# Quarter-block products mixed with whole ones, weight sums by accumulating transfers, and stored low parts, in a decoder layer on one core

## The chip, the cores and the metric

The kernel runs on one core of one Trainium2 chip, as one program. The time is the device time of one execution in microseconds; before the change it is the median of three runs. The engines are named as in the profile: PE (TensorE matmuls, with PEld for its weight loads), DVE (VectorE), ACT (ScalarE), POOL (GpSimd) and SP (SyncE). SP and POOL issue the transfers here, each in the order of its own queue (q1 in the profile is SP's queue, q0 POOL's); both run on the same 16 DMA engines.

## The reference

One layer, 2048 tokens of width 1024, in float32:

```python
h = x * (1.0 + sc1) + sh1                      # sc, sh, g: from cond @ w_ada + b_ada
z = h @ w_in[l]                                # 1024 -> 2048
y_conv = gate_b * _short_conv(gate_c * v_conv, conv_w[l])
y_pool = _multiscale_pool(v_pool, w_pool[l], pool_scale[l])
mix = jnp.concatenate([y_conv, y_pool], axis=-1) @ w_out[l]
x = _layer_norm(ALPHA * x + (1.0 + g1) * mix, ln1_g[l], ln1_b[l])
h = x * (1.0 + sc2) + sh2
f = jnp.square(jax.nn.relu(h @ w_mlp_in[l])) @ w_mlp_out[l]   # 1024 -> 4096 -> 1024
x = _layer_norm(ALPHA * x + (1.0 + g2) * f, ln2_g[l], ln2_b[l])
```

## The kernel before

The tokens go through in two blocks of 1024 (`b` 0 and 1). Each block passes the input projection, the convolution and pooling, the output projection with the first normalisation, the up-projection in eight groups of 512 hidden channels (`up`), and the down-projection with the second normalisation (`down`).

Every float32 operand is split into a high and a low part (`split`: a copy on ACT, line 81, and a subtraction on DVE, line 82), and a product takes three matmuls (`mm3`, lines 86 to 88): high by high, high by low, low by high. Most of the large products are done as seven half-size products in place of eight, in the manner of Strassen and Winograd. `ORDER` lists the seven: number 0 is block 11 by block 11, 1 is 12 by 21, 2 to 5 take sums s1 to s4 of the left operand's blocks and sums 1 to 3 of the weights, or block 22, and 6 takes block 22 and sum 4. Sums of weights are made once, by loading four blocks, four DVE operations and four stores.

In the second block's down-projection three of the seven products (`FINE`: 1, 5 and 3, here numbered n = 0, 1, 2) are cut once more into seven, so that they become 21 parts with matmuls of 256 columns (line 1139). Their left operands are quarter blocks that `up` stores in `uquart` as it goes (`save_quarters`). Their weight sums, `wquart`, are made by `sum_quarters` during the second block's up-projection: `QUARTER_SUMS` says how many of the twelve calls follow each group. A call loads four half rows on SP (line 980) into two `o` tiles, makes four DVE operations (line 91) and stores four results on POOL (line 992). The weights of n = 0 and 1 are an input (`w2q`); those of n = 2 are the first block's weight sums (`w2sum`).

The second block's down-projection runs product 0 in two halves of four groups, then the 21 parts one behind the other, then products 2, 4 and 6, each in two halves. In its second half such a product goes tile by tile (`by_tile`), so that each of the four output tiles ends, and is added and normalised, while the next one is multiplied. Product 0, 2, 4 and 6 share four banks, on which each adds to what stands there; the parts use three others. Loads of operands run one half, or two parts, ahead.

`residual` loads the eight saved rows of the first normalisation (`nsave`) on SP into `r` tiles, scales and shifts them on DVE, and stores them (`rsave`) on POOL. It is driven in four turns of two rows from `down`.

The order on each engine is not only that of the source. The framework lists the program's instructions by readiness and priority and gives each engine a fixed list; `issue_after` holds an instruction back behind another one of its engine. On the chip each engine works its list in order and waits where an operand, a tile or a place among its outstanding transfers isn't there. Tiles come from pools of fixed size: 28 `h` tiles for split operands, 12 `o`, 6 `w`, 5 `r`, of 512 KiB each, and 8 banks `ps`.

The first input projection (`first_group`) opens the program: for each of eight steps SP loads two rows of `wada`, a strip of `win0` and one of `xT` (line 101), DVE makes the dot products for scale and shift and the low parts, and PE does 24 matmuls (line 402). POOL's first transfer is a row of `wada` for a later scale (line 205).

## Time and profile before

| | |
|---|---|
| median of 3 runs | 1771.32 us (1770.84 to 1772.63) |
| profiled execution | 1769.99 us, span 1768.2 us |
| PE busy | 1733.0 us (98%), 8132 matmuls |
| DVE, ACT, POOL busy | 1374.6, 887.1, 253.6 us |
| transferred | 497 MB; q1 324 MB, q0 171 MB |
| DMA engines' share, first 60 us / 60 to 200 us | 0.97 / 0.92 |

The page gives busy time by engine; the view by stretches gives, for each stretch, its length and then for each engine the busy time and in brackets the count of instructions, the granted TensorE clock (1.00 is full), the share of the 16 DMA engines that was in use, and GB/s. The view of waits gives who waited for whom: total, times, longest. A row of the timeline is start, length, engine, line, operation, output and input tiles; in brackets the idle time before and what ended it. A group's row gives count, busy time and mean ns of one, then the idle time before them.

### The profile page before, as it was taken

Reading aid. Unit: us, or ns where it says so; the run is one execution under the profiler, and the core shown is the slowest. Engines: PE = TensorE matmul, PEld = TensorE weight load, DVE = VectorE, ACT = ScalarE, POOL = GpSimd, SP = SyncE. Lnnn points to the kernel's source line nnn. Section 1 sums busy time; section 2 is a strip of 40 time slices with the busy share of each in tenths; the row PEclk is TensorE's granted clock in tenths of the full one; section 3 lists DMA queues with packets and bytes.
Section 4 is the critical chain, followed back from the end, with each engine's and each line's share of the span. In section 5 each row is a group of like instructions: output and inputs, shape, how many; then the busy total and the mean of one; then the engine's idle time right before and its main releaser. Section 6 shows DMA issues by size and latency. Waiting matters only on the chain.

```text
span 1768.2 us, 22793 instructions
## 1 busy us (share of the span) xinstructions
PE 1733.0 (98%) x8132; PEld 1453.7 (82%) x8132; DVE 1374.6 (78%) x1820; ACT 887.1 (50%) x1206; POOL 253.6 (14%) x469
## 2 busy tenths in 40 slices
PE   9999999999999999999999999999999999799997
PEld 8888888888888888888888888888877778799886
DVE  7997788877677866677786887887777668888895
ACT  5322368544445555445763345855444362666451
POOL 0222220123222000000000010112333221000000
PEclk9999999999999999999999999999999999899999
DMA  9899766788888997877653384755777799999781
GB/s 386 337 346 331 297 239 247 293 298 329 322 327 298 402 395 290 316 250 249 215 190 114 107 286 161 262 217 219 273 269 266 271 381 386 382 347 342 262 299 48
DMA packets 159841, 497.27 MB, mean 281 GB/s; under 512 B 18544, under 2 KB 26224, under 8 KB 159728
## 3 DMA queue, kind: packets, MB, share of 16 engines
q1 hardware_dynamic: 110768, 324.36, 50.5%
q0 software_dynamic: 48960, 171.47, 25.3%
q8 instruction: 63, 1.03, 0.2%
q14 instruction: 50, 0.41, 0.1%
HBM read 339.00 MB, written 156.76 MB: 280 GB/s over the span
## 4 chain that ended last, share of the span: by engine, by line
PE 82%; DVE 6%; DMA 5%; issue 4%; SPq 2%; ACT 1%; POOL 0%; DVEq 0%; ACTq 0%; POOLq 0%
PE ps L87 24%; PE ps L86 24%; PE ps L88 24%; PE ps L1139 6%; DVE o L91 3%; PE ps L402 2%; SPq L980 2%; DMA o<-in_w2q 1%; DVE w L82 1%; DMA r<-in_w 1%; DMA o<-w2sum 1%; PE ps L753 1%; DVE r L91 1%; DVE h L82 1%; DMA rsave<-r 0%
## 5 line engine op out<-in xcount | busy, mean ns | idle before, releaser
L86 PE MATMUL ps<-h,w 128*128 128x512 f32 x1312 | 511.7, 391 | 9.9 <-ACT o L1006 9.9
L88 PE MATMUL ps<-h,w 128*128 128x512 f32 x1312 | 512.1, 391 | 1.5 <-DVE w L82 1.5
L87 PE MATMUL ps<-h,w 128*128 128x512 f32 x1312 | 511.8, 390 | 0.0
L86 PE MATMUL ps<-h,h 128*128 128x512 f32 x928 | 361.8, 390 | 0.0
L88 PE MATMUL ps<-h,h 128*128 128x512 f32 x928 | 361.6, 390 | 0.0
L87 PE MATMUL ps<-h,h 128*128 128x512 f32 x928 | 361.5, 390 | 0.0
L81 ACT CAST h<-r 128x1024 fp32r<-128x1024 f32 (+1 forms) x202 | 205.5, 1021 | 243.9 <-PE ps L87 118.0
L82 DVE TENSOR_TENSOR h<-r,h 128x1024 fp32r<-128x1024 f32 (+1 forms) x202 | 238.6, 1186 | 80.8 <-ACT h L81 80.1
L86 PEld LDWEIGHTS ps<-h,w 128*128 128x128 f32 x1312 | 246.9, 188 | 63.2 <-ACT o L1006 11.6
L88 PEld LDWEIGHTS ps<-h,w 128*128 128x128 f32 x1312 | 247.1, 188 | 53.7 <-DVE w L82 2.7
L87 PEld LDWEIGHTS ps<-h,w 128*128 128x128 f32 x1312 | 247.2, 188 | 51.5 <-DVE h L82 0.4
L81 ACT CAST w<-r 128x1024 fp32r<-128x1024 f32 x156 | 163.5, 1052 | 224.2 <-PE ps L87 217.4
L82 DVE TENSOR_TENSOR w<-r,w 128x1024 fp32r<-128x1024 f32 x156 | 190.2, 1222 | 87.1 <-ACT w L81 86.4
L91 DVE TENSOR_TENSOR o<-o,o 128x512 f32<-128x512 f32 (+2 forms) x246 | 200.2, 823 | 25.0 <-DMA usum<-o 18.6
L86 PEld LDWEIGHTS ps<-h,h 128*128 128x128 f32 x928 | 174.3, 188 | 36.2 <-DVE o L91 0.3
L88 PEld LDWEIGHTS ps<-h,h 128*128 128x128 f32 x928 | 174.3, 188 | 36.1
L87 PEld LDWEIGHTS ps<-h,h 128*128 128x128 f32 x928 | 174.3, 188 | 35.9
L82 DVE TENSOR_TENSOR h<-w,h 128x1024 fp32r<-128x1024 f32 x130 | 158.7, 1221 | 11.5 <-ACT h L81 11.4
L91 DVE TENSOR_TENSOR o<-o,ps 128x512 f32<-128x512 f32 (+1 forms) x174 | 112.9, 657 | 54.9 <-PE ps L88 50.4
L1139 PE MATMUL ps<-h,h 128*128 128x256 f32 x1008 | 130.0, 293 | 12.9 <-DVE h L82 6.9
L1139 PEld LDWEIGHTS ps<-h,h 128*128 128x128 f32 x1008 | 127.9, 201 | 15.0 <-DVE h L82 8.0
L81 ACT CAST h<-w 128x1024 fp32r<-128x1024 f32 x130 | 136.5, 1050 | 6.4 <-DMA w<-in_w 4.9
(148 smaller groups left out, 1418.3 us busy)
## 6 DMA issues: line engine op xcount, KB each, us to landing
usum<-o POOLq DMA_DIRECT2D x88, 512.0 KB, 4.0
r<-usum SPq DMA_DIRECT2D x88, 512.0 KB, 5.4
w<-w2sum SPq DMA_DIRECT2D x62, 512.0 KB, 6.2
r<-in_w SPq DMA_DIRECT2D x60, 512.0 KB, 6.0
r<-uquart SPq DMA_DIRECT2D x42, 512.0 KB, 6.4
o<-in_w SPq DMA_DIRECT2D x72, 256.0 KB, 5.8
w2sum<-o POOLq DMA_DIRECT2D x64, 256.0 KB, 5.8
w<-in_w SPq DMA_DIRECT2D x32, 512.0 KB, 6.0
```

The source lines that it names most:

```text
L81: high = nc.scalar.copy(hi, src)
L82: return high.ins, nc.vector.tensor_tensor(lo, src, hi.bitcast(F32), op=ALU.subtract).ins
L86: nc.tensor.matmul(ps, whi, xhi, start=first, stop=False, skip_group_check=goes_on)
L87: nc.tensor.matmul(ps, whi, xlo, start=False, stop=False, skip_group_check=goes_on)
L88: nc.tensor.matmul(ps, wlo, xhi, start=False, stop=last, skip_group_check=goes_on)
L91: return nc.vector.tensor_tensor(out_, a, b_, op=op)
L402: nc.tensor.matmul(ps[m, h], wt[:, w : w + P], A[k][p // 2][:, hs], start=k == 0 and p == 0, stop=k == KD - 1 and p == 2)
L753: nc.tensor.transpose(ps[:, t * P : t * P + P], R[4 * h + t][:, k * P : k * P + P], ident)
L980: nc.sync.dma_start(r, weight_quarter(n, i, hf, some))
L1139: nc.tensor.matmul(ps, a[:, us], w[:, gs], start=not begun, stop=hf == 1 and g == 3 and a is ul, skip_group_check=True)
```

## The change

- **Mixed order.** In the second block's down-projection products 0 and 2 are issued by single groups of 512 channels, two times eight of them, and mixed with the 21 parts by a string (`MIX`, 1 is a group, 0 a part). Operands are made ahead as long as no more than 28 `h` tiles are held. Product 2 ends with its last group, no longer tile by tile. Products 4 and 6 follow as before.
- **Weight sums by transfers.** `sum_quarters` no longer loads, adds and stores: for each product n it issues, from POOL, eight plain copies from HBM to HBM (step 0) and eight copies that add to what stands at the target (steps 1 to 3, `accum_op`). Since these only add, some signs change: s1 and s4 of the quarter blocks, and how three of the parts are added to the output (`fine_less`, `fine_from`). The calls stand in the source in the second block's input projection (`SUM_TURNS`) and output projection. A call that adds waits for the step before it.
- **Stored low parts.** In the first block, the low parts of the weights of products 4 and 6 (16 tiles) are stored (`wlow`, POOL); in the second they are loaded on SP in place of the DVE subtraction.
- **Residual rows** of the second block are loaded from POOL's queue into `o` tiles, in place of SP and `r` tiles.

```diff
-QUARTER_SUMS = (0, 1, 2, 2, 2, 2, 2, 1)
+MIX = "1110101010101000100100100101001001001"
...
+            for n, step in SUM_TURNS[j]:
+                sum_quarters(n, step)
...
+    SUM_TURNS = (((0, 0),), ((1, 0), (0, 1)), ((2, 0), (1, 1), (0, 2)), ((2, 1), (1, 2), (0, 3)))
...
+        if b:
+            sum_quarters(2, 2)
+            sum_quarters(1, 3)
         matmuls(4, Y, False, every, first_row)
...
+        if b:
+            sum_quarters(2, 3)
         matmuls(6, X, False, every, last_row)
...
-    def sum_quarters(n, hf, part_):
-        a, b_ = t_o(T), t_o(T)
-        b22, b12, b11, b21 = a[:, :H], a[:, H:], b_[:, :H], b_[:, H:]
-        for i, r in ((3, b22), (1, b12), (0, b11), (2, b21)):
-            load_quarter(r, n, i, hf, slice(2 * part_, 2 * part_ + 2))
-        tt(b22, b22, b12, ALU.subtract)
...
+    SUM_STEPS = (((0, 1), (2, 1), (1, 3), (3, 2)), ((0, 0), (2, 3)), ((1, "0"),), ((3, "1"),))
+
+    def sum_quarters(n, step):
+        for hf in range(2):
+            for i, what in SUM_STEPS[step]:
+                src = quarter_sum(n, hf, int(what)) if what in ("0", "1") else weight_quarter(n, what, hf)
+                if step:
+                    nc.gpsimd.dma_start(quarter_sum(n, hf, i), src, accum_op=ALU.add,
+                                        max_dma_last_dim=4096)
+                else:
+                    nc.gpsimd.dma_start(quarter_sum(n, hf, i), src)
...
-                done = split(src, hi, lo)
+                if b and src is q and i in LOWS:
+                    nc.sync.dma_start(lo.bitcast(F32), wlow[LOWS[i], g])
+                    nc.scalar.copy(hi, src)
+                else:
+                    done = split(src, hi, lo)
+                    if not b and src is q and i in LOWS:
+                        nc.gpsimd.dma_start(wlow[LOWS[i], g], lo.bitcast(F32))
...
-            r = t_r()
-            nc.sync.dma_start(r, nsave[t])
+            r = t_o(D) if b else t_r()
+            (nc.gpsimd if b else nc.sync).dma_start(r, nsave[t])
...
+        units = [("h", i, hf) for i in ((4, 6) if b else (0, 1, 2, 3, 5, 4, 6)) for hf in range(2)]
+        if b:
+            parts_ = [("f", k, m) for k in FINE for m in range(7)]
+            groups = [("c", i, g) for i in (0, 2) for g in range(NC)]
+            mixed_ = []
+            for n in MIX:
+                mixed_ += [groups.pop(0) if n == "1" else parts_.pop(0)]
+            units = mixed_ + units
+        size = {"c": 4, "f": 8, "h": 16}
...
+            while ahead_ < len(units) and (
+                    ahead_ <= n + 1 or b and held + size[units[ahead_][0]] <= 28):
+                made.append(operands(*units[ahead_]))
+                held += size[units[ahead_][0]]
+                ahead_ += 1
```

How it moves instructions, at three places. The first is the start of POOL's list, where `vhalo` is one of the tiles cleared at the opening, `ident` the unit matrix for transposes, and `msum` takes the stores of the first mixing group. Before:

```order
L166 MEMSET vhalo 128x64
masks.py:199 ISA
masks.py:199 AFFINE_SELECT ident<-ident 128x128
L205 DMA h_857<-in_wada 128x1024
L341 DMA msum<-o_555 128x2x512
```

And with the change:

```order
L166 MEMSET vhalo 128x64
L1000 DMA wquart<-in_w2q 16x8192
masks.py:199 ISA
masks.py:199 AFFINE_SELECT ident<-ident 128x128
L1000 DMA wquart<-in_w2q 16x8192 x15
L997 DMA wquart<-in_w2q 128x1024 x8
L997 DMA wquart<-wquart 128x1024 x8
L206 DMA h_858<-in_wada 128x1024
L342 DMA msum<-o_556 128x2x512
```

The copies and the adding copies of n = 0 and 1, which the source has in the second block, stand at the very head, 32 transfers of 512 KiB, one of them ahead of the unit matrix; those of n = 2 stand behind the first block's `w2sum` stores.

The second place is SP's list where the second block's down-projection starts (`usum` holds the up-projection's results, `in_w` are weights of product 0, `in_rows` the two rows that scale the residual). Before:

```order
L1076 DMA w_11659<-in_w 128x1024
L1093 DMA r_11675<-nsave 128x1024
L980 DMA w_11796<-in_w2q 128x1024
L1093 DMA r_11680<-nsave 128x1024
L980 DMA w_11808<-in_w2q 128x1024
L980 DMA o_11551<-w2sum 128x2x256 x2
L980 DMA o_11552<-w2sum 128x2x256 x2
L210 DMA o_11669<-in_rows 128x1024
L210 DMA o_11671<-in_rows 128x1024
L1093 DMA r_11685<-nsave 128x1024
L1093 DMA r_11690<-nsave 128x1024
L1117 DMA r_11795<-uquart 128x1024
```

And with the change:

```order
L1145 DMA w_11507<-in_w2q 128x1024
L1145 DMA w_11519<-in_w2q 128x1024
L1086 DMA w_11532<-in_w 128x1024
L1145 DMA w_11575<-in_w2q 128x1024
L1145 DMA w_11587<-in_w2q 128x1024
L1086 DMA w_11636<-in_w 128x1024
L1143 DMA w_11732<-wquart 128x1024
L211 DMA o_11542<-in_rows 128x1024
L1141 DMA r_11518<-uquart 128x1024
L1084 DMA r_11530<-usum 128x1024
L211 DMA o_11544<-in_rows 128x1024
L1141 DMA r_11574<-uquart 128x1024
```

The residual rows (`nsave`) and the last weight sums (`o` from `w2sum`) are gone from SP's list, loads for groups (`in_w`, `usum`) and for parts (`in_w2q`, `wquart`, `uquart`) alternate, and the second half of the first part (`r_11518`) stands behind the first of the two scaling rows.

The third place is DVE's list where product 2 of the second block ends (`ps_11546` to `ps_11549` are its four banks, `bc` is the gate's row). With the change:

```order
L91 TENSOR_TENSOR o_11462<-o_11462,ps_11546 128x512
L91 TENSOR_TENSOR o_11462<-o_11462,bc_4836 128x1024
L91 TENSOR_TENSOR o_11463<-o_11463,ps_11547 128x512
L1350 SCALAR_TENSOR_TENSOR o_11462,mv_13701<-o_11462,r_13698 128x512 x2
L91 TENSOR_TENSOR o_11463<-o_11463,bc_4836 128x1024
L735 TENSOR_SCALAR mv_13701<-mv_13701 128x1
L1350 SCALAR_TENSOR_TENSOR o_11463,mv_13732<-o_11463,r_13729 128x512
L1360 SCALAR_TENSOR_TENSOR o_13708<-o_11462,mv_13701,w_13704 128x1024
```

Before, splits for the next product (`h_13695`, `h_13703`, `h_13707`) stand between the first tile's operations:

```order
L91 TENSOR_TENSOR o_11565<-o_11565,ps_11695 128x512
L82 TENSOR_TENSOR h_13695<-w_13688,h_13694 128x1024
L82 TENSOR_TENSOR h_13703<-r_13698,h_13702 128x1024
L91 TENSOR_TENSOR o_11565<-o_11565,bc_4835 128x1024
L82 TENSOR_TENSOR h_13707<-w_13700,h_13706 128x1024
L91 TENSOR_TENSOR o_11566<-o_11566,ps_11696 128x512
L91 TENSOR_TENSOR o_11566<-o_11566,bc_4835 128x1024
L1317 SCALAR_TENSOR_TENSOR o_11565,mv_13750<-o_11565,r_13747 128x512 x2
```

With the change the four tiles' operations stand close behind one another, and the adds of the third and fourth bank behind most of the first two tiles' work.

More of the change, by code (lines that the diff above doesn't have):

```diff
@@ L1103, in down, with operands @@
         lo_, hi_ = halves
-        coarse = (0, 2, 4, 6) if b else (0, 1, 2, 3, 5, 4, 6)
-        steps = [(i, hf) for i in coarse for hf in range(2)]
-        def operands(n):
-            i, hf = steps[n]
-            return down_operands(i, range(4 * hf, 4 * hf + 4))
+        units = [("h", i, hf) for i in ((4, 6) if b else (0, 1, 2, 3, 5, 4, 6)) for hf in range(2)]
[7 more added lines that the diff above has]
+        size = {"c": 4, "f": 8, "h": 16}
+        def operands(kind, i, n):
+            if kind == "f":
+                return fine_operands(i, n), None
+            return down_operands(b, i, [n] if kind == "c" else range(4 * n, 4 * n + 4))
         def fine_operands(i, m):
@@ L1378, in mlp @@
                     sums += [(sum_weights, wins[0], winsum, p) for p in halves]
-        else:
-            quarters = [(n, hf, p) for n in range(3) for hf in range(2) for p in range(2)]
         for g in range(NC):
```

112 lines of the change are left out of this document (52 added, 60 removed).

## The prediction

> **What bounds the kernel now.** I read the page first, then busy time by stretches, then TensorE's own waits.
>
> ```profile
> span 1768.2 us, 22793 instructions
> PE 1733.0 (98%) x8132; PEld 1453.7 (82%) x8132; DVE 1374.6 (78%) x1820; ACT 887.1 (50%) x1206; POOL 253.6 (14%) x469
> L1139 PE MATMUL ps<-h,h 128*128 128x256 f32 x1008 | 130.0, 293 | 12.9 <-DVE h L82 6.9
> ```
>
> TensorE (PE) is the bound: what it loses is lost for good, and the change leaves its list of matmuls equal in number. So the question is only how many microseconds PE loses before and after. The stretches (length, then busy time and count for PE, PEld, DVE, ACT and POOL, granted clock, DMA share, GB/s) tell where:
>
> ```profile
> 0.00:60.00 60.00, 58.19 (x265) 48.63 (x266) 46.85 (x92) 35.34 (x51) 2.05 (x26) 1.00 0.97 388
> 60.00:200.00 140.00, 140.00 (x623) 116.08 (x622) 123.64 (x192) 38.14 (x50) 41.44 (x74) 1.00 0.92 343
> 350.00:700.00 350.00, 350.00 (x1550) 290.11 (x1549) 254.05 (x286) 180.68 (x205) 64.76 (x121) 1.00 0.88 332
> 650.00:830.00 180.00, 180.00 (x799) 149.23 (x799) 127.63 (x147) 88.35 (x114) 9.05 (x17) 1.00 0.81 294
> 1250.00:1450.00 200.00, 188.57 (x812) 153.65 (x811) 143.58 (x190) 94.61 (x113) 57.13 (x96) 0.98 0.76 283
> 1450.00:1650.00 200.00, 187.08 (x1262) 175.25 (x1261) 165.22 (x170) 115.52 (x137) 11.83 (x20) 0.96 0.99 367
> 1550.00:1600.00 50.00, 50.00 (x419) 50.00 (x419) 40.21 (x42) 34.48 (x43) 0.00 (x0) 1.00 0.98 345
> 1650.00:1742.00 92.00, 92.00 (x407) 76.02 (x406) 67.00 (x93) 37.58 (x60) 0.00 (x0) 1.00 0.59 210
> ```
>
> From 350 to 700 us a matmul of 512 columns takes 350/1550 = 0.226 us; a quarter-block matmul (256 columns) takes 50/419 = 0.119 us. At these rates the 812 matmuls from 1250 to 1450 are 183.4 us of work, so 16.6 us are lost there (the second block's up-projection). From 1450 to 1650 it is 1008 x 0.119 + 254 x 0.226 = 177.7 us, so 22.3 us are lost, around the start of the quarter-block products. Elsewhere PE runs at its pace. **All that this change can win is therefore 39 us**, and only in that last fifth. The other thing to see is the front: in the first 200 us the transfers' share is 0.97 and 0.92. There PE is not waiting, but the 16 DMA engines have next to no room.
>
> **The front: what the accumulating transfers cost there.** In the order of the changed kernel, 32 transfers stand at the head of POOL's queue: 16 plain ones from the stored weights to the quarter sums, and 16 accumulating ones, for the first two of the three products. They read inputs only, so nothing holds them back; before, POOL sent nothing until 36.7 us. They meet the opening loads on SP's queue.
>
> ```profile
> 36.70 0.67 POOL L205 DMA_DIRECT2D h<-in_wada  x1 [34.75 <-DVE h L196]
> 9.56 44.20 PE L402 MATMUL ps<-h,w 128*128 128x512 f32 x192 [0.74 <-ACT h L218]
> 28.60 1.55 SPq L101 DMA_DIRECT2D h<-in_wada  x2
> 31.72 0.33 SPq L101 DMA_DIRECT2D o<-in_xT  x1
> o<-in_xT SPq DMA_DIRECT2D x7, 512.0 KB, 8.8
> q1 hardware_dynamic: 7176, 22.70, 95.0%
> GB/s 418 415 415 410 426 421 421 415 407 412 431 421 426 421 421 421 410 426 421 421 421 410 426 421 421 431 404 377 421 421 421 411 408 419 423 426 410 423 259 83
> ```
>
> These are POOL's first transfer, PE's eight opening steps, SP's last loads for step 7 with their median time to landing, SP's queue over the first 60 us (95% of the engines' time), and the rate from 30 to 60 us, about 420 GB/s. A pass of 512 KiB at that rate takes 0.524 MB / 420 GB/s = 1.25 us. How two full queues share is seen from 190 to 198 us:
>
> ```profile
> q0 software_dynamic: 584, 2.12, 65.0%
> q1 hardware_dynamic: 585, 1.17, 37.6%
> ```
>
> Packet for packet: 584 of POOL's queue against 585 of SP's. By the end of step 7 SP has sent about 32 transfers (four to a step), POOL's head has 32, so nearly all of POOL's must pass before step 7's operands are in. The opening is therefore late by the whole time of POOL's 32 transfers, less the lead of the loads. The lead: the last load of step 7 lands at 31.72 + 8.8 = 40.5 us, PE starts that step at 9.56 + 7/8 x 44.20 = 48.2 us; 8 us. I count it in full, though DVE's work on the step also comes out of it.
>
> The trace of before has no transfer from HBM to HBM and no accumulating one, so both prices are bounds. A plain copy takes at least one pass, and at most two, as if it were a load and then a store: 1.25 to 2.5 us. An accumulating transfer may cost no more than a pass, and at most three (source in, old sum in, new sum out): 1.25 to 3.75 us. I take the middles, one and a half and two passes, since the rows speak for neither end: 16 x 1.25 x (1.5 + 2) = 70 us, less 8, so **+62 us**. Both ends for the range: 16 x 1.25 x 2 - 8 = 32 us and 16 x 1.25 x 5 - 8 = 92 us. PE does not win this back: from there it is busy all the time.
>
> The Trainium skill, page "DMA: Bandwidth & Descriptors", section "Latency and other measured facts", gives 207 to 214 GB/s in each direction for copies between two tensors in HBM. By it, as an estimate, a 512 KiB copy takes 2.5 us, my upper bound; the copies would be 40 us instead of 30, and the forecast 10 us later. No run here shows such a copy yet, so the middle stays in the sum.
>
> The third product's sums need the first block's weight sums. They go out between about 350 and 700 us: 8 plain and 8 accumulating transfers, 35 us at the same prices, where the share of 0.88 leaves 0.12 x 350 = 42 us. The 16 stores of low parts (16 x 1.25 = 20 us) go into 650 to 830 us, where 0.19 x 180 = 34 us are free. If that cover were gone they would cost up to those 35 and 20 us. POOL also waits in its queue for each accumulating step while stores of the up-projection stand behind it, and output tiles come free later; PE has been without any wait there. I take **+1 us** (0 to 8) for all this.
>
> **The back: what is won.** PE's waits after 1250 us, then DVE's and ACT's in the up-projection:
>
> ```profile
> PE ps L86 <- ACT o L1006: 9.9, 4, 3.0
> PE ps L1139 <- DVE h L82: 6.9, 4, 4.0
> PE ps L1139 <- ACT h L81: 6.0, 3, 2.6
> PE ps L88 <- DVE w L82: 1.5, 2, 1.3
> DVE o L91 <- DMA o<-in_w2q: 17.5, 8, 3.9
> ACT o L1015 <- DVE o L91: 58.1, 15, 8.3
> ```
>
> PE waits for ACT's copies out of its banks (L1006), ACT waits behind DVE, and DVE stands still for the loads of the old weight sums (o<-in_w2q). Those loads, 48 DVE operations and 48 POOL stores leave this stage. In the first block's up-projection, where the same stage stands without them, PE waits for nothing. So I give back 16 of the 16.6 us: **-16 us** (12 to 16.6).
>
> For the quarter-block start these rows matter: the first such matmul, a DVE operation held by a store of the same tile, the last store of quarter blocks, the split waiting for the quarter blocks' load, and a residual load's time to landing.
>
> ```profile
> 1485.53 1.72 PE L1139 MATMUL ps<-h,h 128*128 128x256 f32 x13
> 1458.82 1.23 DVE L91 TENSOR_TENSOR o<-o,o 128x1024 f32<-128x1024 f32 x1 [4.21 <-DMA usum<-o]
> 1463.96 0.75 POOL L970 DMA_DIRECT2D uquart<-o  x1 [2.33 <-DVE o L91]
> 1488.23 1.04 ACT L81 CAST h<-r 128x1024 fp32r<-128x1024 f32 x1 [7.64 <-DMA r<-uquart]
> r<-nsave SPq DMA_DIRECT2D x16, 512.0 KB, 6.2
> ```
>
> Product 0 took 192 x 0.226 = 43.4 us and so began at 1442.1. In the change the first quarter part comes after three of its eight groups, at 1442.1 + 3 x 5.4 = 1458.3. Its second half needs group 7's quarter blocks, whose splits stand on DVE behind the operation of 1458.8 and four short ones, so end at about 1464; PE has 2.9 us of first half to do and waits some 2 us. The next group's weight split stands behind the first residual operation, whose load now stands on POOL's queue behind the store of 1463.96: 1463.96 + 0.75 + 6.2 = 1471, with two operations of 1.2 us 1473.4. PE is there at 1466.5, and waits 7. So 9 of the 22.3 us stay. After that the mix has room: 21 parts of 5.7 us and 16 groups of 5.4 us are 207 us and move 21 x 4 + 16 x 2 + 16 (residual) transfers of 0.524 MB, 69 MB, or 335 GB/s against 420.
>
> At the end of product 2 the change loses its order by output tile, so four tiles end within 5.4 us where they ended 5.4 us apart. DVE's operations per tile, from 1640 to 1742 us:
>
> ```profile
> L91 DVE TENSOR_TENSOR o<-o,bc 128x1024 f32<-128x1024 f32 (+1 forms) x8 | 7.6, 956 | 0.1
> L91 DVE TENSOR_TENSOR o<-o,ps 128x512 f32<-128x512 f32 x8 | 5.5, 684 | 10.1 <-PE ps L88 10.1
> L1317 DVE SCALAR_TENSOR_TENSOR o<-o,r 128x512 f32<-128x512 f32 x8 | 5.4, 683 | 0.0
> L1327 DVE SCALAR_TENSOR_TENSOR o<-o,mv,w 128x1024 f32<-128x1024 f32 x4 | 5.1, 1280 | 0.0
> ```
>
> 0.7 + 1.2 + 2 x 0.7 + 1.3 + 1.3 = 5.9 us a tile. Product 4 adds on the same banks; PE's order lets it work on the first two for about 10 us, and the adds of banks three and four stand some 14 and 20 us behind the last quarter part. PE waits about 3 + 1 = 4 us there, which is new. So of 22.3 us there stay 9 + 4, and **-9 us** (-20 to +2) is won. The 16 splits that the stored low parts save on DVE win nothing of themselves: from 1650 to 1742 PE is busy for 92 of 92 us; their loads (20 us) lie in 41% free transfer time.
>
> **Sum**, against the profiled execution's 1769.99 us (span 1768.2): 1770.0 + 62 + 1 - 16 - 9 = 1808.0. That execution lies 1.3 us under the median of the three runs, 1771.32, so **1809 us**.
>
> **Rivals.** *Faster: the front absorbs the copies.* Copies that never touch the core's own memory may use a part of the engines that loads leave free, or the queue may get to them only when SP's is dry. For it: no row shows such a copy. Against it: 584 to 585, and 0.97. At half a pass for each transfer the front is 16 x 1.25 x 1 - 8 = 12 us, and 1770 + 12 + 1 - 25 = 1758 (1759 as a median). It turns at a front of 24 us: 32 us of transfer time, one microsecond a transfer. With no collision at all it is 1747, the case that the order does not hold on the chip.
>
> *Worse: the dear end, and POOL's queue as a second brake.* Three and two passes give 92 us; POOL's later loads of w_ada rows then leave so late that DVE, which has their dot products in line before weight splits, stands some 10 us. 1770 + 102 + 1 - 25 = 1848.
>
> *The back wins nothing beyond the up-projection*: eight residual tiles, each through POOL's queue, hold DVE again and again; the 9 us turn into a loss of 10: 1827. For it: DVE is at 165 of 200 us there. Against it: later residual loads leave early.
>
> **Chances.** Forecast 0.68 (own range 1777 to 1838, from the two ends of the front), faster rival 0.17, worse 0.09, back lost 0.06. Below about 1760 lies most of the faster rival, above 1846 half of the worse one: range 1760 to 1846. A measurement tells 0.2% (3.5 us) from no change; a front of 20 to 28 us would give that, 0.04, taken from the forecast's low end. Faster 0.17, same 0.04, slower 0.79.
>
> **What would show it.** In the profile after: POOL's queue busy with wquart from 2 us on; PE's opening matmuls stretched from 44 us to about 100 with idle time before them put down to DVE or ACT and loads; full transfers until past 100 us; each later stage late by the same amount; no PE wait from 1250 to 1450 us in old terms; waits at the first quarter part and behind product 2 of 9 and 4 us. If the opening's matmuls end before about 75 us, the prices of the copies are wrong and so is the sign.

## The result, and the profile after

The change made the kernel slower: median 1828.33 us (1825.45 to 1830.66) against 1771.59 us before, measured beside it; the ratio is 1.0319, 95% interval 1.0301 to 1.0337. The profiled execution has a span of 1823.6 us, 55.4 us more than before. Two rows of its page, and TensorE's own waits in the whole execution (total, times, longest):

```profile
span 1823.6 us, 22633 instructions
PE 1741.1 (95%) x8132; PEld 1455.6 (80%) x8132; DVE 1329.2 (73%) x1756; ACT 894.0 (49%) x1206; POOL 276.2 (15%) x493
```

```profile
PE ps L403 <- ACT h L219: 43.5, 6, 14.2
PE ps L88 <- DVE w L82: 10.8, 3, 9.4
PE ps L86 <- ACT o L1014: 4.5, 2, 3.6
PE ps L403 <- DVE h L91: 4.3, 1, 4.3
PE ps L1164 <- ACT h L81: 3.5, 1, 3.5
```

PE has the same 8132 matmuls and 95% in place of 98%. Most of its new waiting is in the opening (L403 was L402 before): for ACT's high parts, which wait for loads. The view by stretches shows where:

```profile
0.00:60.00 60.00, 25.99 (x95) 20.47 (x96) 14.54 (x36) 10.67 (x16) 18.34 (x52) 0.68 0.98 304
60.00:160.00 100.00, 84.98 (x354) 68.96 (x353) 73.13 (x127) 34.84 (x50) 17.35 (x28) 0.90 1.03 351
500.00:750.00 250.00, 233.46 (x1012) 191.54 (x1011) 166.81 (x187) 119.74 (x135) 51.11 (x85) 0.97 0.98 347
1310.00:1500.00 190.00, 189.00 (x834) 156.23 (x833) 126.65 (x163) 92.36 (x110) 41.52 (x65) 1.00 0.52 184
```

Only 95 matmuls fall into the first 60 us, where 265 did. From 500 to 750 us, in the first block's up-projection, PE is busy 233 of 250 us, where it had no gap. The second up-projection (1310 to 1500) loses 1 us of 190, at a transfer share of 0.52.

The waits are not the whole loss. PE is busy 8.1 us longer for the same matmuls: in the opening those behind a wait ran slower. Two rows of PE's timeline show it:

```profile
88.20 8.21 PE L403 MATMUL ps<-h,w 128*128 128x512 f32 x24 [7.58 <-ACT h L219]
96.75 16.66 PE L403 MATMUL ps<-h,w 128*128 128x512 f32 x72 [0.33 <-ACT h L219]
```

The 24 matmuls behind a wait of 7.6 us took 8.21 us, at a granted clock of 0.68; the 72 behind them, nearly without a wait, took 5.55 us for each 24, at 1.00.

Since PE's list is the same up to the second down-projection, the same matmul can be timed in each trace. This table gives how many microseconds later it starts than before (negative: earlier); a step between two columns is what was lost there. The head is its start before the change, the last column is the last matmul.

| kernel | 20.1 | 100.1 | 500.0 | 720.1 | 960.2 | 1110.1 | 1440.2 | end 1758.8 | median us |
|---|---|---|---|---|---|---|---|---|---|
| the change | 31.1 | 59.6 | 74.6 | 80.6 | 84.2 | 84.0 | 68.9 | 55.4 | 1828.3 |
| `held_all` | -0.6 | -0.6 | -0.7 | -0.7 | 5.9 | 58.9 | 43.0 | 31.3 | 1799.3 |
| `held_01` | -0.8 | -0.8 | 14.9 | 19.4 | 26.4 | 45.2 | 30.1 | 16.6 | 1789.6 |
| `held_2` | 31.1 | 59.3 | 59.3 | 59.3 | 63.9 | 82.5 | 67.1 | 54.1 | 1825.2 |
| `front_plain` | 28.1 | 39.2 | 56.5 | 62.9 | 68.7 | 68.6 | 53.6 | 41.9 | 1812.9 |
| `front_4k` | 8.3 | 53.4 | 70.5 | 78.3 | 81.8 | 81.6 | 66.2 | 54.0 | 1823.2 |
| `n2_free` | -0.2 | -0.2 | 7.6 | 8.8 | 13.7 | 33.6 | 18.7 | 7.5 | 1777.1 |
| `n2_plain` | -0.8 | -0.8 | 8.8 | 12.8 | 16.7 | 34.7 | 19.6 | 5.6 | 1781.5 |
| `no_sums` | -0.5 | -0.5 | -0.1 | -0.1 | 6.4 | 6.2 | -8.3 | -21.9 | 1746.0 |
| `spread` | -0.4 | -0.4 | 0.0 | 0.0 | 3.5 | 5.4 | -9.3 | -18.5 | 1753.7 |
| `spread2` | -0.2 | -0.2 | 0.2 | 0.2 | 5.5 | 7.8 | 0.2 | -10.7 | 1758.5 |
| `spread_nomix` | -0.1 | -0.1 | 0.2 | 0.2 | 5.2 | 5.9 | -6.7 | -11.3 | 1756.5 |
| `spread_nolow` | -0.5 | -0.5 | -0.2 | -0.2 | 1.8 | 4.7 | -10.3 | -19.0 | 1750.7 |

For the change: 59.6 lost in the opening (47.8 of it waits of L403, the rest slower matmuls), 15.0 + 6.0 in the first block's up-projection, 3.6 around the change of blocks; then 15.1 won in the second up-projection and 13.5 behind it. POOL's timeline shows what happened in the first two places (start, length, engine, line, operation, tiles; in brackets the idle time before and what ended it; the last row is DVE's):

```profile
1.77 0.64 POOL L1000 DMA_DIRECT2D wquart<-in_w2q  x1
...
20.32 0.49 POOL L1000 DMA_DIRECT2D wquart<-in_w2q  x1 [2.00 <-DMA wquart<-in_w2q]
21.81 0.88 POOL L997 DMA_DIRECT2D wquart<-in_w2q  x1 [1.01 <-DMA wquart<-in_w2q]
...
79.08 0.81 POOL L997 DMA_DIRECT2D wquart<-wquart  x1 [3.03 <-DMA wquart<-wquart]
98.59 0.59 POOL L206 DMA_DIRECT2D h<-in_wada  x1 [18.69 <-DVE h L197]
...
502.44 2.95 POOL L1000 DMA_DIRECT2D wquart<-w2sum  x4 [0.25 <-issue]
516.07 1.23 POOL L997 DMA_DIRECT2D wquart<-w2sum  x1 [10.68 <-DMA wquart<-w2sum]
...
527.64 0.83 POOL L997 DMA_DIRECT2D wquart<-wquart  x1 [8.15 <-DMA wquart<-w2sum]
528.20 0.85 POOL L1030 DMA_DIRECT2D usum<-o  x1
536.88 0.85 POOL L997 DMA_DIRECT2D wquart<-wquart  x1 [7.83 <-DMA wquart<-wquart]
537.43 2.45 POOL L1030 DMA_DIRECT2D usum<-o  x4
547.47 1.83 DVE L91 TENSOR_TENSOR o<-o,o 128x1024 f32<-128x1024 f32 x2 [12.94 <-DMA usum<-o]
```

The 32 transfers at the head are issued from 1.8 to 79 us, and the first `wada` row leaves at 98.6 in place of 36.7. At 502 us the third product's sums start. Each step waits for the landing of the one before: 10.7, 8.2 and 7.8 us of POOL's time. The up-projection's stores (`usum<-o`) stand behind them, four go out together at 537.4, DVE waits 12.9 us for their tiles, and PE's wait of 9.4 us for a low part (`w` L82), which ends at 554.7, follows from that.

### The profile page after: what moved, and what is told of

It reads as the page before. It is cut to its first block, busy times and chain, and to the rows that moved or that the text cites. A ratio compares the mean times of both kernels' runs of the same rounds, so it can differ in the third digit from the quotient of the medians.

```text
span 1823.6 us, 22633 instructions
## 1 busy us (share of the span) xinstructions
PE 1741.1 (95%) x8132; PEld 1455.6 (80%) x8132; DVE 1329.2 (73%) x1756; ACT 894.0 (49%) x1206; POOL 276.2 (15%) x493
## 4 chain that ended last, share of the span: by engine, by line
PE 79%; DMA 12%; DVE 3%; issue 3%; ACT 2%; POOL 1%; SPq 0%; DVEq 0%; POOLq 0%; ACTq 0%
PE ps L87 24%; PE ps L88 24%; PE ps L86 24%; PE ps L1164 7%; DMA o<-in_xT 5%; DMA r<-usum 2%; DVE o L91 1%; PE ps L403 1%; DMA wquart<-w2sum 1%; PE ps L758 1%; DMA w<-in_w 1%; DVE h L82 1%; DMA usum<-o 1%; DMA winsum<-o 1%; DMA r<-in_xT 0%
## 5 line engine op out<-in xcount | busy, mean ns | idle before, releaser
L81 ACT CAST h<-r 128x1024 fp32r<-128x1024 f32 (+1 forms) x202 | 205.5, 1021 | 244.4 <-PE ps L87 105.6
L82 DVE TENSOR_TENSOR h<-r,h 128x1024 fp32r<-128x1024 f32 (+1 forms) x202 | 238.2, 1184 | 94.3 <-ACT h L81 92.1
L81 ACT CAST w<-r 128x1024 fp32r<-128x1024 f32 x156 | 164.4, 1054 | 265.7 <-PE ps L87 256.8
L82 DVE TENSOR_TENSOR w<-r,w 128x1024 fp32r<-128x1024 f32 x156 | 190.6, 1222 | 119.0 <-ACT w L81 117.5
L91 DVE TENSOR_TENSOR o<-o,o 128x1024 f32<-128x1024 f32 (+2 forms) x238 | 202.5, 862 | 48.8 <-DMA usum<-o 40.7
L82 DVE TENSOR_TENSOR h<-w,h 128x1024 fp32r<-128x1024 f32 x114 | 139.0, 1219 | 15.4 <-ACT h L81 15.4
L81 ACT CAST h<-w 128x1024 fp32r<-128x1024 f32 x114 | 119.7, 1050 | 24.4 <-DMA w<-in_w 14.5
L1164 PE MATMUL ps<-h,h 128*128 128x256 f32 x1008 | 126.1, 286 | 4.5 <-ACT h L81 3.5
```

The source lines that it names most:

```text
L81: high = nc.scalar.copy(hi, src)
L82: return high.ins, nc.vector.tensor_tensor(lo, src, hi.bitcast(F32), op=ALU.subtract).ins
L91: return nc.vector.tensor_tensor(out_, a, b_, op=op)
L1164: nc.tensor.matmul(ps, a[:, us], w[:, gs], start=not begun, stop=hf == 1 and g == 3 and a is ul, skip_group_check=True)
```

## The experiments

**Where the sums run.** Theory: the loss comes from where the sums stand in POOL's list; the gain at the end is real. `stored[0]` is the last mixed store of the latest group of the second block's first layer. (The sums are 48 transfers, 24 that copy and 24 that add, where the expectations speak of 40.)

```diff
-        nc.gpsimd.dma_start(msum[6, j], v[:, :H])
+        stored[:] = [nc.gpsimd.dma_start(msum[6, j], v[:, :H]).ins]
...
     def sum_quarters(n, step):
+        with tc.issue_after(stored[0]) if n in (0, 1, 2) else nullcontext():
```

For all three products this is `held_all`:

> The 40 sums of quarter blocks keep their work and their number but are held behind the mixed stores of the second block's first layer, so that none is issued before about 1000 us (at 1000 to 1250 us the transfer engines of the changed kernel are busy 0.26 to 0.77 of the time). Theory (the changed kernel's loss is 59 us at 0 to 100 us, where the early sums share the transfers packet for packet with the opening's loads, and 24 us at 500 to 700 and 950 to 1000 us, where the sums of the third product stand in POOL's list ahead of the up-projection's stores; the 28 us gained at the end are real): 1828 - 59 - 24 = 1745 us, faster than before by 1.5%; a few us more if the last sums now delay the loads of x that stand behind them in POOL's list. Rival A (the sums cost the same wherever they run, since it is their traffic that costs): 1815 to 1830. Rival B (the gain at the end depends on the stretched opening, or on sums that are long done): 1765 to 1775, no better than before.

1799.32 us, ratio 1.0164 (1.0149 to 1.0180). 29 us faster than the change, but not the 83 expected. The opening and the up-projection are as before (the table: -0.7 at 720 us); 53 us are lost anew between 960 and 1110 us. The waits of TensorE and DVE there, then POOL's timeline:

```profile
PE ps L86 <- DVE o L879: 29.5, 2, 28.2
DVE o L879 <- DMA o<-in_x: 29.3, 1, 29.3
```

```profile
1075.91 1.15 POOL L1003 DMA_DIRECT2D wquart<-w2sum  x1 [8.30 <-issue]
1091.59 1.17 POOL L1003 DMA_DIRECT2D wquart<-w2sum  x1 [14.53 <-issue]
1092.21 3.94 POOL L1003 DMA_DIRECT2D wquart<-wquart  x4
1094.81 2.99 POOL L862 DMA_DIRECT2D o<-in_x  x3
```

The rows of x that the output projection adds (`o<-in_x`) stand in POOL's list behind the sums. They leave from 1095 us on; DVE has been waiting since 1082 and goes on at 1111.5. So the sums took a loss to the next place where something stood behind them. The profile names no cause for POOL's own waits of 8.3 and 14.5 us (`issue`), and the engines are full there too, 1.02 from 1050 to 1100 us, so the list and the traffic are not told apart here. Neither my theory's number nor rival A's (1815 to 1830) came out; the theory had put the loads of x behind the sums at a few microseconds.

`held_01` holds the first two products alone (`n in (0, 1)`), `held_2` the third (`n in (2,)`):

> Only the sums of the first two products, which read the input, are held to the second block; those of the third stay where they are in the changed kernel. Theory: the opening is as before, 1828 - 59 = 1769 us, and the gaps of PE at 500 to 700 us, 20 us more than before, stay. Rival A (traffic costs the same anywhere): 1815 to 1830. A third reading, that the gaps at 500 to 700 us come from a heap order that the stretched opening upsets, gives 1745 to 1750.

> Only the sums of the third product are held to the second block; the first two products' sums stay at the head of POOL's list. Theory: 1828 - 24 = 1804 us, with no PE gap above 2 us between 500 and 700 us, and the opening's 59 us kept. If the gaps at 500 to 700 us have another cause than these sums (the stored low parts, the order of the list): 1825 to 1830.

1789.62 us (ratio 1.0106, 1.0091 to 1.0121) and 1825.24 us (1.0310, 1.0293 to 1.0327). `held_01` is free of the opening's loss, keeps the third product's (20 us by 720 us), and pays 7 between 720 and 960 and 19 between 960 and 1110: 1790 where 1769 was expected. `held_2` loses nothing from 100 to 720 us, so these 21 us do belong to the third product's sums; it pays 19 between 960 and 1110 (63.9 to 82.5) instead, and comes out at 1825 for 1804. 1825 is what the expectation gave to another cause, but the gap that the theory had named is gone, and the loss stands elsewhere. In `held_01` the new loss isn't the list of the rows of x: DVE waits for `o<-in_x` for 2.6 us only. There the engines are full where before they were not, and ACT waits for SP's loads. The stretch from 1080 to 1100 us, before and in `held_01`, and ACT's largest group of waits in `held_01` from 1030 to 1110 us (total, times, longest):

```profile
1080.00:1100.00 20.00, 20.00 (x90) 16.56 (x89) 14.16 (x38) 12.02 (x35) 1.69 (x4) 1.00 0.29 107
1080.00:1100.00 20.00, 14.16 (x54) 10.83 (x55) 17.80 (x22) 7.25 (x12) 5.91 (x10) 0.91 1.05 283
ACT h L81 <- DMA r<-msum: 28.5, 5, 11.9
```

So by these rows the traffic, rival A's idea, has a part in it. Moving is no gain by itself.

**What all the sums cost.** `no_sums` leaves them out; the three products are computed from raw quarters.

```diff
-                    nc.sync.dma_start(q, wquart[n, hf, int(w) - 1])
+                    nc.sync.dma_start(q, w2q[n % 2, int(w) - 1, hf])
...
-            for n, step in SUM_TURNS[j]:
-                sum_quarters(n, step)
```

> The changed kernel without any of the sums of weight quarters: no transfer fills them, and the parts that would load them load the input's raw quarters instead (the same size), so that the three quarter-block products are computed from other weights. It shows what the rest of the change is worth (the parts alternating with whole groups, the stored low parts, no DVE sums in the second up-projection). Theory: the whole loss is the sums', 1828 - 59 - 24 = 1745 us, with PE's opening and 500 to 700 us as before the change, and no stretch at 1000 to 1150 us, where the held sums lost 50 us. Rival (part of the loss at 500 to 700 or 950 to 1000 us is the stored low parts' or the new order's): 1755 to 1770.

1746.0 us, ratio 0.9862 (0.9847 to 0.9877), as expected. So the sums as placed cost 1828.3 - 1746.0 = 82 us, and all the rest of the change, with DVE freed of the sums, is worth 25 us.

**Spread out.** `spread` keeps every sum, with the plain copies of the first two products behind the stores of the first two groups of the second block's input projection, and the other steps, one or two at a time, each behind the last store of a group of the second up-projection (there `stored[0]` is also set by the quarter-block stores).

```diff
-    SUM_TURNS = (((0, 0),), ((1, 0), (0, 1)), ((2, 0), (1, 1), (0, 2)), ((2, 1), (1, 2), (0, 3)))
+    SUM_TURNS = (((0, 0),), ((1, 0),), (), ())
+    SUM_UPS = (((0, 1),), ((1, 1),), ((0, 2), (1, 2)), ((0, 3), (1, 3)), ((2, 0),), ((2, 1),), ((2, 2),), ((2, 3),))
...
     def sum_quarters(n, step):
+        with tc.issue_after(stored[0]):
```

> All 40 sums are kept, one step at a time in POOL's list: the plain copies of the first two products behind the stores of the second block's first two groups, then one or two steps behind the stores of each of the eight groups of the second up-projection, so that each step's source landed a group (37 us) earlier and the loads of x have none of them ahead. Theory A (what costs is a transfer on POOL that waits for the one before and keeps the stores and loads behind it waiting): no waits are left, 1745 to 1752 us, faster than before by 1 to 1.5%. Theory B (what costs is the traffic itself, whose time the transfer engines lack): the copies and adds take 24 x 1.4 + 24 x 2.6 = 96 us of all 16 engines, and the engines of the kernel before are busy 0.50 to 0.78 at 1000 to 1400 us, so some 110 us are free there: between 1755 and 1790.

1753.74 us, ratio 0.9907 (0.9890 to 0.9923): faster than the kernel before by 0.9% and than the change by 4%, and between the two ranges, 2 us above A's and 1 below B's. The same stretch of the second block without the sums (`no_sums`), and with them (`spread`):

```profile
1150.00:1400.00 250.00, 250.00 (x1103) 206.63 (x1103) 183.60 (x232) 128.82 (x152) 55.18 (x87) 1.00 0.52 187
```

```profile
1150.00:1400.00 250.00, 250.00 (x1104) 206.60 (x1103) 180.33 (x230) 128.49 (x151) 80.15 (x115) 1.00 0.81 247
```

```profile
1252.57 3.46 POOL L1000 DMA_DIRECT2D wquart<-wquart  x4
1255.44 1.16 POOL L1033 DMA_DIRECT2D usum<-o  x1
```

The transfer share rises from 0.52 to 0.81 and PE stays busy 250.00 of 250 us. The last rows are `spread`'s POOL timeline: four adding transfers are issued with no wait, as what they read landed a group earlier, and the next store follows. POOL isn't free of waits everywhere: among the third product's transfers it still stands for 5.0 us (at 1339 us) and 9.2 us (at 1381 us), but PE is busy 100.00 of 100 us from 1300 to 1400.

`spread2` puts more of them earlier (both products' copies at the first group, their first sums at the second, then mostly one step per group, the last group free):

```diff
-    SUM_TURNS = (((0, 0),), ((1, 0),), (), ())
+    SUM_TURNS = (((0, 0), (1, 0)), ((0, 1), (1, 1)), (), ())
-    SUM_UPS = (((0, 1),), ((1, 1),), ((0, 2), (1, 2)), ((0, 3), (1, 3)), ((2, 0),), ((2, 1),), ((2, 2),), ((2, 3),))
+    SUM_UPS = (((2, 0),), ((0, 2),), ((2, 1),), ((1, 2),), ((2, 2),), ((0, 3), (1, 3)), ((2, 3),), ())
```

> The spread run with other places: both products' copies behind the stores of the first group of the second block's first layer and their first sums behind the second group's (without any sum, the transfer engines are busy only 0.23 to 0.39 at 925 to 1025 us), the rest one step behind each of the first seven groups of the second up-projection and none behind the last, whose end runs into a stage busy 0.96 to 1.03. Theory A (with no wait on the list and free transfer time the sums cost nothing): the 7.7 us between the spread run and the one without sums go to 0 to 3: 1746 to 1750. Theory B (what is left is the adding's own slowness beside the loads, wherever it is): 1753 to 1760.

1758.50 us, ratio 0.9929 (0.9913 to 0.9946): theory A missed. PE loses one stretch of 5 us behind the first group of the second up-projection, where the third product's eight copies now stand (POOL's timeline with one row of DVE's, and PE's waits, of `spread2`, 1200 to 1260 us):

```profile
1189.95 3.70 POOL L1003 DMA_DIRECT2D wquart<-w2sum  x5
...
1201.15 0.71 POOL L1003 DMA_DIRECT2D wquart<-w2sum  x1 [3.99 <-DMA wquart<-w2sum]
1201.76 0.64 POOL L1033 DMA_DIRECT2D usum<-o  x1
1206.23 0.74 POOL L971 DMA_DIRECT2D uquart<-o  x1 [3.83 <-DVE o L91]
1207.34 0.57 POOL L973 DMA_DIRECT2D uquart<-o  x1 [0.36 <-DMA wquart<-w2sum]
1225.27 1.23 DVE L91 TENSOR_TENSOR o<-o,o 128x1024 f32<-128x1024 f32 x1 [12.68 <-DMA usum<-o]
```

```profile
PE ps L86 <- ACT o L1017: 5.1, 1, 5.1
```

Even with no step before them, eight transfers at once hold up POOL's list. The stores behind wait for their landings, DVE waits 12.7 us for a store, ACT waits for DVE (12.4 us), and PE for ACT.

**What the transfers themselves cost.** In `front_plain` the first two products' adding transfers only overwrite; in `front_4k` the plain copies are cut into 4 KB pieces as well.

```diff
-                    nc.gpsimd.dma_start(quarter_sum(n, hf, i), src, accum_op=ALU.add,
-                                        max_dma_last_dim=4096)
+                    nc.gpsimd.dma_start(quarter_sum(n, hf, i), src, max_dma_last_dim=4096,
+                                        **({"accum_op": ALU.add} if n == 2 else {}))
```

```diff
-                    nc.gpsimd.dma_start(quarter_sum(n, hf, i), src)
+                    nc.gpsimd.dma_start(quarter_sum(n, hf, i), src, max_dma_last_dim=4096)
```

> As the changed kernel, but the 16 transfers of the first two products that add to what stands in memory only overwrite it (the same sizes, the same pieces of 4 KB, the same order, the sums left out, so two of the products are computed from other weights). Prices the adding itself. Theory: in the changed kernel a 4 KB packet that adds takes 0.327 us on a transfer engine against 0.16 of a plain one, 16 x 128 / 16 = 128 packets per engine x 0.167 = 21 us of the opening: about 1807 us. Rival: the time of a packet that adds is hidden behind the other queue's, and the loss is a matter of how many packets alternate: 1822 to 1830. Second rival: adding also delays through the order of the steps (each waits for the one before): down to 1795.

> The changed kernel with the plain copies too cut into pieces of 4 KB, as those that add; same bytes, same places. In the changed kernel the copies' packets are of about 16 KB, and one of them goes between two of the opening's 4 KB packets, so the opening's loads get 31 to 62 GB/s at 10 to 30 us. Theory (the engines serve the two queues packet for packet): while the copies run the opening gets half, its early stall shrinks, but the same bytes have to go before the opening is over, so most of the 59 us stays: 1815 to 1828. Rival (the size of the pieces is the cause): 1790 or less. Opposite rival (more pieces, more cost for each): 1835 to 1850.

1812.86 us (1.0244, 1.0225 to 1.0262) and 1823.15 us (1.0293, 1.0275 to 1.0310). Without the adding the opening is 39.2 us late in place of 59.6: the adding costs 20 us there, close to the 21 expected; 15 of them are left in the whole time, since the later stages lost some microseconds more, so the whole time is 6 us above the theory's 1807. With small pieces the first matmuls are 8 us late in place of 31 (column 20.1), but by 100 us it is 53.4: the same bytes have to pass, as the theory has it. The copies' packets were not of 16 KB but of 32 KB (16 rows of 8192 numbers): half of the packets of POOL's queue carry 4 bytes and halved the mean. The queues over 38 us in which the change adds, and over 20 us in which `front_plain` overwrites (packets, MB, share of 16 engines):

```profile
q0 software_dynamic: 1485, 5.37, 70.9%
q1 hardware_dynamic: 1483, 4.90, 34.7%
```

```profile
q0 software_dynamic: 1046, 4.24, 55.2%
q1 hardware_dynamic: 1053, 3.33, 43.3%
```

One packet for one in both. A packet of POOL's takes 0.709 x 16 x 38 / 1485 = 0.29 us in the first and 0.552 x 16 x 20 / 1046 = 0.17 in the second. These are means over packets of all sizes; in the packet records those of 4 KB took 0.327 us where they add and 0.159 us where they overwrite.

**Why the third product's sums cost 20 us in the first block.** `n2_plain` is `held_01` with the third product's adding transfers only overwriting, their waits kept. `n2_free` writes them to places of their own, neither adding nor waiting for each other.

```diff
-                    nc.gpsimd.dma_start(quarter_sum(n, hf, i), src, accum_op=ALU.add,
-                                        max_dma_last_dim=4096)
+                    nc.gpsimd.dma_start(quarter_sum(n, hf, i), src, max_dma_last_dim=4096,
+                                        **({"accum_op": ALU.add} if n < 2 else {}))
```

```diff
+                if n == 2 and step:
+                    nc.gpsimd.dma_start(wspare[hf, i].rearrange("p (g n) -> p g n", n=Q), weight_quarter(n, i, hf))
+                    continue
```

> As the run that holds the first two products' sums to the second block, with the third product's 16 transfers at their place in the first block's up-projection, but each copies a quarter of the stored sums to a place of its own without adding (same bytes, 1 KB pieces), so none waits for another; the third product is computed from other weights. That run lost 16 us at 450 to 500 and 4 at 550 to 650 us. Theory A (the chain of waits between the steps on POOL's list holds the stores behind them): these 20 us go, 1790 - 20 = 1770 us. Theory B (traffic in a stage whose transfer engines are busy 0.80 to 0.95 of the time): most stays, 1780 to 1790.

> As the run that holds the first two products' sums (1789.6 us), with the third product's transfers at their places and with their waits for each other, but the 8 that add only overwrite (third product computed from other weights). The run in which these transfers neither add nor wait for each other gave 1777 us and 9 us of loss at 450 to 700 us in place of 20. This one keeps the waits and takes the adding alone away. If the waits in POOL's list are the other half: 1784 to 1790, PE loss 15 to 20 us. If the adding's slower packets are: 1775 to 1780, loss 8 to 11 us.

1777.14 us (1.0039, 1.0022 to 1.0056) and 1781.48 us (1.0056, 1.0037 to 1.0074). The profiled execution of `n2_plain` lies under its median, so I go by the table's column at 720 us, where all three can be compared. There `held_01` has lost 20 us (19.4 + 0.8), `n2_plain` 13.6, `n2_free` 9.0. So in these three executions some 6 to 7 us go with the adding, 4 to 5 with the steps' waits for each other, and 9 stay when both are gone; the medians, 8 and 4 us apart, give the same order. Neither theory alone holds. The first difference isn't the adding's alone: the adding transfers that read the stored sums move in packets of 1 KB, 0.101 us each, which is 3.2 us of all engines for 512 KiB, and without the adding the same transfers, like the copies, move in packets of 4 KB. In `n2_free` POOL still stands 7.0 us before the eighth of its eight transfers, though those before it already read the same stored sums, and from 443 to 466 us the two queues together fill the engines (timeline, then queues):

```profile
455.76 0.71 POOL L1003 DMA_DIRECT2D wspare<-w2sum  x1 [7.02 <-DMA wquart<-w2sum]
463.26 0.56 POOL L1040 DMA_DIRECT2D usum<-o  x1 [6.79 <-ACT o L1034]
```

```profile
q0 software_dynamic: 1271, 4.55, 65.4%
q1 hardware_dynamic: 1140, 2.88, 36.0%
```

How these 9 us divide between the full engines and the list isn't known.

**The other parts, on `spread`.** `spread_nomix` takes the alternating back, `spread_nolow` the stored low parts.

```diff
-MIX = "1110101010101000100100100101001001001"
+MIX = "1111111100000000000000000000011111111"
```

```diff
-    LOWS = {4: 0, 6: 1}
+    LOWS = {}
```

> The run with the sums spread over the second block (1753.7 us), with the order of the second block's down-projection undone: all eight groups of the first whole product, then the 21 quarter-block parts, then the eight groups of the second, as the kernel before has them but for its place of two groups; operands are still fetched as far ahead. Prices the alternating. Theory (alternating the parts with whole groups gives the quarter parts' operands time, worth the 9 us that the prediction gave it or the 13 that the traces show between 1450 and 1550 us): 1763 to 1767 us, with PE waiting on h at the first quarter parts. Rival (the gain is the fetching ahead, or the sums taken from DVE, not the order): 1750 to 1757.

> The spread run without the stored low parts: the second block computes the low parts of the weights of products 4 and 6 again on DVE (16 subtractions of 128x1024) and moves 16 MB less. Theory of the prediction (low parts cost nothing where they are stored and remove the wait of 4 us between products 2 and 4): 1755 to 1758 us. Rival A (DVE has room, so they change nothing): 1752 to 1755. Rival B (the transfer engines are full at 1450 to 1700 us, so the 8 MB of loads cost more than the subtractions saved): 1745 to 1751.

1756.54 us (0.9919, 0.9902 to 0.9936) and 1750.74 us (0.9888, 0.9873 to 0.9902), beside `spread`'s 1753.74 (0.9907, 0.9890 to 0.9923). The intervals overlap. The alternating is worth perhaps 3 us and not the 9 to 13 expected: after the second up-projection PE wins 9.2 us with it and 4.6 without (table, last two columns), and PE's wait for operands at the quarter parts tells the same. The first row is of `spread_nomix`, the others of `spread`:

```profile
PE ps L1167 <- DVE h L82: 11.2, 3, 6.5
```

```profile
PE ps L1167 <- ACT h L81: 3.5, 1, 3.5
PE ps L1167 <- DVE h L82: 2.0, 2, 1.1
```

The stored low parts bring nothing; the kernel without them is the fastest of all that compute the layer, though its lead over `spread` is not certain. Its median lies in rival B's range, but B's cause is not seen: behind 1440 us it wins 8.7 us where `spread` wins 9.2, and the two traced executions end within 0.5 us of each other.

## Why the prediction was right, and which term was mis-sized

Slower was forecast with 1809 us; it is 1828.3, inside the range of 1760 to 1846. By its terms, predicted and measured (from the table's first row): the front +62 and +59.6; the third product's sums and the low parts +1 and +24.4 (59.6 to 84.0); the second up-projection -16 and -15.1; the quarter-block start and the mix -9 and -13.5. The sums are +38 and +55.4. **The term that was mis-sized is the +1 for the third product's sums and the low parts, by 23 us**; the others were off by 1 to 5.

- *The front: right in size, by a mechanism that the rows bear out.* One packet for one, all 32 transfers ahead of step 7. That the middles between the bounds came so near the measured prices was luck: no row had shown a price. The prices can now be read in `spread`, where the copies and the adds each run nearly alone: POOL's queue from 958 to 972 us, with eight copies, and the rate from 1192 to 1204 us, about the first ten of which are four adding transfers:

```profile
q0 software_dynamic: 505, 4.66, 97.1%
...
GB/s 150 191 191 205 232 205 205 205 178 219 164 164 177 205 177 205 205 164 178 205 205 191 218 205 205 218 191 219 205 205 205 205 191 218 218 260 355 423 396 423
```

  0.524 MB / 4.66 MB x 14 x 0.97 = 1.53 us a copy, and 0.524 MB / 205 GB/s = 2.56 us an add. (About 1 MB of the 4.66 are the mixing group's last stores; the copies' own packets of 32 KB, 16 to a copy, took 1.44 us each, which is 1.44 us of all 16 engines.) I had taken 1.88 and 2.5. With the measured prices 16 x (1.53 + 2.56) - 8 = 57 us, and 59.6 were lost; the lead of 8 us counted in full was about right. `held_01` and `held_all` show it from the other side: no transfer at the head, no loss.
- *The Trainium skill, "DMA: Bandwidth & Descriptors", section "Latency and other measured facts"*, gives 207 to 214 GB/s in each direction for copies of tiles of 128 rows of 16 KiB on the sync and scalar queues, and less at other distances of the rows, which the prediction leaves out. As an estimate that made 2.5 us and a forecast 10 us later. The trace does not agree for the copies here, 16 rows of 32 KB from POOL's queue: over the window of 14 us they and the stores moved at 341 GB/s, 1.53 us a copy. No run here has the page's layout.
- *The faster rival* (the front absorbs the copies, a microsecond a transfer or less) fell by these prices and by 59.6 us. *The worse rival* fell too: an add took 2.56 us and not 3.75, and `held_2` loses nothing between 100 and 500 us, where POOL's late loads were to stop DVE. *The rival of the back* fell by the 13.5 us that were won there.
- *The own range*: its low end comes out at 1778, 30 under 1808.0, where the prediction has 1777.
- *The third product's sums.* I set 35 us of transfers against 42 us that the engines have free between 350 and 700 us, a mean over the stage. But they come in two bunches of eight, and within a bunch the engines are full: 1.02 from 500 to 540 us and 1.05 from 630 to 675, where the mean from 500 to 750 is 0.98. I had named the queue behind them ("POOL also waits in its queue for each accumulating step while stores of the up-projection stand behind it") and put nothing on it, because PE had been without any wait there. The timeline shows that chain, POOL to the `usum` stores to DVE to PE, and `held_2` shows that the 21 us by 720 us are these sums'. `n2_plain` and `n2_free` divide them: adding (with its smaller packets), waiting, and a rest whose cause stays open.
- *The low parts* are a part of the same term. Between 720 and 960 us the change loses 3.6 us, but `no_sums` loses 6.5 and, without low parts, `spread_nolow` 2.0. Whether the low parts cost any of that is not shown.
- *The second up-projection* came out as forecast, -15.1 for -16. Of PE's waits there only 1 us is left.
- *The quarter-block start.* Of the waits forecast for the mix (9 us at the first parts, 4 behind product 2) the first part's are there (3.5 us for `h` L81 among them), but none came behind product 2. So 13.5 us were won and not 9. Of the 22.3 us that the prediction saw lost here only 12.9 were waits (PE is busy 187.08 of 200 us in its row); the rest were slower matmuls, at a granted clock of 0.96 in the same row. In the same way the gain is 8.4 us of waits (12.9 before, 4.5 after) and 5.1 us of busy time, 306.2 against 301.1 us for the last 1786 matmuls. That the alternating is the cause is not shown: without it half of the gain stays on `spread`.
- *The signs for which to look*: POOL busy with `wquart` from 1.8 us, and full transfers past 100 us, were there; the opening's matmuls ended at 113 us, where about 100 was said.

The best version is not the change but its sums put where their sources are old and transfers are idle: 1753.7, or 1750.7 without the low parts.

## What to carry to other kernels

A sum made by transfers, without a compute engine, is not free: price its passes, then ask what stands behind it in the list of its queue's engine, and whether that stretch, not the stage's mean, has idle transfer time. A step that reads the result of the step before should be issued a whole group of work later, when that result has landed. Moving a group of such transfers as a whole moved its loss, to the list behind it (`held_all`) or to the loads beside it (`held_01`); only taking it apart removed most of it here (82 us to 8).

## What the runs showed of the hardware that was not expected

- A transfer that adds in HBM moved 205 GB/s of its own bytes, 2.56 us for 512 KiB over all 16 engines; a plain copy from HBM to HBM took 1.44 to 1.53 us (`spread`).
- Cutting copies from packets of 32 KB to 4 KB changed who waits first, 31 to 8 us at the 89th matmul, but the lateness after the opening only by 6 us of 60. The two queues alternate packet for packet, so the queue with the larger packets takes the larger share: from 12 to 30 us of the change POOL's 316 packets, about half of them of 4 bytes, carried 5.21 MB and SP's 314 carried 0.85. The Trainium skill, "DMA: Bandwidth & Descriptors", section "Queues, rings and completion order", says that each engine goes round its queues by packets; 1485 packets against 1483 in the rows above agree.
- Eight transfers issued together, none of which reads another's result, still stopped POOL for 7 us (`n2_free`); the profile puts the end of that wait down to the landing of an earlier one.
- A wait of PE cost more than its length: behind it the matmuls ran slower (8.21 us for 24 at a granted clock of 0.68, 5.55 at 1.00). In the opening that is 12 of the 59.6 us.
